# A one-core decoder layer in split float32: the last two products of each column of weight blocks in the same order as all others

## The chip, the core and the metric

The kernel runs on one core of a Trainium2 chip, as one program. The metric is the device time of one execution in microseconds (us), the median of three runs. The engines of the core are TensorE (PE in the profile, its weight loads PEld), VectorE (DVE), ScalarE (ACT), GpSimd (POOL) and SyncE (SP, which starts the transfers).

## What is computed

One layer of a hybrid decoder on 256 tokens of width 2048, in float32: a combined projection, two kinds of attention, gates, an output projection, a wide feed-forward part with a convolution of width 3, and a gated embedding at the end. Cut to what matters here, it is a chain of matrix products:

```python
u = rmsnorm(h, g_mix_pre)
proj = u @ w_in                       # q, k, v of 16 heads, two gates
ya = dilated_mixture_attention(...) @ w_branch_a
yb = stick_breaking_attention(...) @ w_branch_b
mix = (sigmoid(gla) * ya + sigmoid(glb) * yb) @ w_out
h = h + rmsnorm(mix, g_mix_post)
u = rmsnorm(h, g_ffn_pre)
up = causal_depthwise_conv(u @ w_up, conv_w, conv_b)
f = (gelu(gate_ff) * value) @ w_down
h = h + rmsnorm(f, g_ffn_post)
h = h + sigmoid(h @ w_ple_gate) * (p @ w_ple_in)
```

## The kernel before

**Split products.** Every float32 factor is held as two parts of a shorter kind (fp32r): a high part, and a low part that is the rest. ACT rounds (L124 for weights, L284 for activations), DVE subtracts (L127, L290, L292). A product of an activation with a weight is high x high + low x high + high x low. An activation tile (u, mg, ft, yT) has for each of its rows k 256 columns of high parts and, behind them, 256 columns of low parts, 512 in all.

**Blocks, columns, tiles.** A weight block is 128x128. The plan lists them in the order in which PE uses them; eight blocks make a tile of 128x1024, which SP loads (raw), ACT turns into hi and DVE into lo. There are 508 tiles, 4064 blocks. All blocks that add up to the same 128 outputs are a column: 16 blocks for most projections, 11 for each quarter of the down projection.

**A block's products.** For most blocks the function mul makes two products. The high one takes the weights' high part against all 512 columns and fills a whole PSUM bank of 512 columns; the low one takes the weights' low part against the first 256 columns and adds to the first half of the bank. Blocks but the last do the high product (L205) and then the low one (L206). The last block of a column does the low one first (L202) and then the high one (L203). mul1 (the branch products, each part's very last column, the small e products; L223 to L225) makes three products of 256 columns, and the v projection three of 512 with the roles exchanged (L436 to L438).

**Order around it.** PE runs the plan in order, column behind column. `mm` is one column; `several` and the loops over a group `first`, `up` or `pg` run three or four columns side by side, row by row, and so end with their last blocks next to each other. A column has a bank of its own, one of four to seven that go round. When a column is done, `both` copies the bank's second half away on ACT (L247) and lets DVE add it to the first half (L250); what follows goes on from there in stages that a queue (`defer`, `due`) hands out, one stage each time PE's program comes to a new tile (`tick`). Ahead of each column's first product PE waits until its bank has been emptied, and ahead of each tile until ACT and DVE have made it. ACT and DVE wait until the buffer that they fill (seven of each) is no longer read.

Of the kernel before, what the change touches and what calls it, by code (L numbers as in the profile page):

```python
# [14 lines left out]
T = 256  # L15
# [77 lines left out]
def hybrid_block_kernel(ctx: ExitStack, tc: tile.TileContext, gx, pT, convp, bias, masks, w, out):  # L93
    nc = tc.nc
    PE, DVE, ACT = nc.tensor, nc.vector, nc.scalar
# [84 lines left out]
    def block(n=1):  # L180

        b = at["block"]
        at["block"] = b + n
        i, c = divmod(b, 8)
        if c == 0:
            tick(i)
        return hi[i][:, c * 128:(c + n) * 128], lo[i][:, c * 128:(c + n) * 128]
# [10 lines left out]
    def mul(ps, rhs, first, last):  # L198

        wh, wl = block()  # L200
        if last:
            PE.matmul(ps[:, :T], wl, rhs[:, :T], start=False, stop=False, skip_group_check=True)  # L202
            PE.matmul(ps, wh, rhs, start=first, stop=True, skip_group_check=True)  # L203
        else:
            PE.matmul(ps, wh, rhs, start=first, stop=False, skip_group_check=True)  # L205
            PE.matmul(ps[:, :T], wl, rhs[:, :T], start=False, stop=False, skip_group_check=True)  # L206

    head = []

# [19 lines left out]
    def bank():  # L229
        pool, bufs = banks["of"][banks["n"] % len(banks["of"])]  # L230
        banks["n"] += 1
        return pool.tile([128, 2 * T], F32, name="mm", bufs=bufs)

    def mm(key, src, fn=mul, ps=None):

        ps = bank() if ps is None else ps
        for _, k, first, last in group(key):
            fn(ps if fn is mul else ps[:, :T], src[:, k], first, last)
        return ps
# [138 lines left out]
    for c, k, first, last in todo:  # L378
        if k == 6:
            at["grow"] = 0.5  # L380
        if c == 0 and 0 < k < KT - 2:
            usplit(u, k + 2, h[:, k + 2], gain(0, k + 2))
        if first:
            mul_first(pss, c, u[:, k])
            continue
        mul(pss[c], u[:, k], first, last)
# [28 lines left out]
    for c in range(len(pss), 8):  # L415
        ps = mm(keys[c], u, ps=spare.pop(0) if spare else None)
# [111 lines left out]
    for s in range(NS):  # L528
        for c in range(8 if s else 0):
            ps = mm(("qk", s, c), u)  # L530
# [46 lines left out]
    for j in range(KT):  # L577
        ps = bank()
# [11 lines left out]
    def several(key, n, src):  # L590
        pss = [bank() for _ in range(n)]
        for c, k, first, last in group(key):
            mul(pss[c], src[:, k], first, last)
        return pss
# [12 lines left out]
    ps = mm(("out", KT - 1), mg, mul1)  # L607
# [103 lines left out]
    for q in range(NQ):  # L711
        for n in range(max(len(pss), q * 2 * QT), (q + 1) * 2 * QT):
            ps = mm(keys[n], u2)
# [4 lines left out]
        for j in range(KT):  # L718
            if q == NQ - 1 and j == KT - 1:
                break  # L720
            ps = down[j] if j < 3 else mm(("down", q, j), ft)
# [7 lines left out]
    ps = mm(("down", NQ - 1, KT - 1), ft, mul1)  # L729
# [24 lines left out]
    for j in range(KT):  # L754
        ps = pss[j] if j < FIRST else mm(("pg", j), u3, mul1 if j == KT - 1 else mul)
# [67 lines left out]
```

## Time and profile before

| what | value |
|---|---|
| median of three runs | 1485.17 us (1484.68 to 1486.23) |
| the profiled execution, whole | 1486.11 us |
| its span, first to last instruction | 1484.3 us |
| PE busy | 1471.9 us, 99% of the span |
| PE's weight loads busy | 1283.7 us, 86% |
| DVE busy | 1035.6 us, 70% |
| ACT busy | 813.0 us, 55% |
| high products on L205 that read u: count, mean | 2448, 400 ns |
| low products on L206 that read u: count, mean | 2448, 281 ns |

The profile lists one execution. Matmuls overlap: a product is listed from its start to its end, and the next one starts before that end, so that the distance from start to start is shorter than the duration. The time that a product costs is therefore read from the starts. A line in order of time has the start, the duration, the engine, the line of the kernel, the operation and its tiles; in brackets stands how long the engine had been idle before it and what released it.

### The profile page before, as it was taken

To read this page: it belongs to the slowest core of one execution; us is meant where nothing else is said; L and a number is where in the kernel's file an instruction comes from. 1 tells how busy PE (TensorE), PEld (TensorE's weight loads), DVE (VectorE), ACT (ScalarE), POOL (GpSimd) and SP (SyncE) were. 2 spreads that over 40 slices of the span, in tenths; PEclk is the share of its full clock that TensorE was granted. 3 is DMA by queue.
4 is the path that set the end of the run, shared out by engine and by line. 5 is a ranking of instruction groups with operands and counts; after the bars stand their busy time and mean duration, and the time that the engine had idled before them with its cause. 6 is when DMAs were issued, how large, how long until landed. Compare 5 with 4: busy or idle time off the path is not lost.

```text
span 1484.3 us, 21918 instructions
## 1 busy us (share of the span) xinstructions
PE 1471.9 (99%) x8425; PEld 1283.7 (86%) x8425; DVE 1035.6 (70%) x1533; ACT 813.0 (55%) x1215; POOL 22.6 (2%) x30
## 2 busy tenths in 40 slices
PE   8999999999999999999999999999999999999998
PEld 7888888888998988978888888888888888888887
DVE  7665555566666655599965778767787677777884
ACT  7454545464455555566654555545555455656562
POOL 0000000000000000020000000000000000000200
PEclk9999999999999999999999999999999999999999
DMA  9645555566566666545765665665656665656381
GB/s 327 214 158 171 174 183 175 182 196 189 187 188 185 185 187 184 168 157 168 221 194 186 185 189 183 192 186 184 186 185 188 191 186 185 185 185 187 111 272 54
DMA packets 78295, 275.11 MB, mean 185 GB/s; under 512 B 8688, under 2 KB 11632, under 8 KB 78192
## 3 DMA queue, kind: packets, MB, share of 16 engines
q1 hardware_dynamic: 78192, 273.73, 59.4%
q8 instruction: 66, 1.08, 0.3%
q14 instruction: 37, 0.30, 0.1%
HBM read 271.60 MB, written 2.10 MB: 184 GB/s over the span
## 4 chain that ended last, share of the span: by engine, by line
PE 96%; DVE 3%; DMA 0%; issue 0%; ACT 0%; SPq 0%
PE mm L205 51%; PE mm L206 26%; PE mm L203 4%; PE mm L436 2%; PE mm L438 2%; PE mm L437 2%; PE mm L202 2%; PE mm L224 1%; PE mm L225 1%; PE mm L223 1%; DVE lo L127 1%; DVE gh L638 1%; PE S L455 1%; PE S L205 0%; DMA raw<-in_w 0%; DVE u L292 0%
## 5 line engine op out<-in xcount | busy, mean ns | idle before, releaser
L205 PE MATMUL mm<-u,hi 128*128 128x512 f32 x2448 | 875.1, 400 | 4.1 <-DVE u L292 2.6
L127 DVE TENSOR_TENSOR lo<-raw,hi 128x1024 fp32r<-128x1024 f32 (+1 forms) x510 | 622.9, 1227 | 182.0 <-ACT hi L124 174.3
L206 PE MATMUL mm<-u,lo 128*128 128x256 f32 x2448 | 688.2, 281 | 0.5 <-DVE lo L127 0.5
L124 ACT ACTIVATE hi<-raw 128x1024 fp32r<-128x1024 f32 (+1 forms) x510 | 534.6, 1053 | 257.6 <-PE mm L205 195.7
L205 PEld LDWEIGHTS mm<-u,hi 128*128 128x128 f32 x2448 | 461.4, 188 | 112.7 <-DVE u L292 3.6
L206 PEld LDWEIGHTS mm<-u,lo 128*128 128x128 f32 x2448 | 463.7, 189 | 6.5 <-DVE lo L127 1.0
L247 ACT ACTIVATE t<-mm 128x256 f32<-128x256 f32 x242 | 91.4, 378 | 248.3 <-PE mm L203 247.9
L205 PE MATMUL mm<-ft,hi 128*128 128x512 f32 x630 | 224.7, 398 | 0.0
L250 DVE TENSOR_TENSOR s<-mm,t 128x256 f32<-128x256 f32 x211 | 89.1, 422 | 129.8 <-ACT t L247 129.8
L206 PE MATMUL mm<-ft,lo 128*128 128x256 f32 x630 | 176.8, 281 | 0.0
L205 PEld LDWEIGHTS mm<-ft,hi 128*128 128x128 f32 x630 | 118.5, 188 | 26.6
L206 PEld LDWEIGHTS mm<-ft,lo 128*128 128x128 f32 x630 | 119.0, 189 | 2.5
L205 PE MATMUL mm<-mg,hi 128*128 128x512 f32 x225 | 80.0, 399 | 0.0
L203 PE MATMUL mm<-u,hi 128*128 128x512 f32 x164 | 65.0, 399 | 0.0
L206 PE MATMUL mm<-mg,lo 128*128 128x256 f32 x225 | 63.2, 281 | 0.0
L693 ACT ACTIVATE cv<-cpad,cw 128x256 f32<-128x256 f32 x88 | 52.6, 598 | 9.1 <-DVE cpad L688 8.7
L436 PE MATMUL mm<-hi,u 128*128 128x512 f32 x128 | 51.1, 400 | 0.0
L205 PEld LDWEIGHTS mm<-mg,hi 128*128 128x128 f32 x225 | 42.3, 188 | 9.9
L438 PE MATMUL mm<-hi,u 128*128 128x512 f32 x128 | 49.9, 390 | 0.0
L437 PE MATMUL mm<-lo,u 128*128 128x512 f32 x128 | 49.8, 389 | 0.0
L202 PE MATMUL mm<-u,lo 128*128 128x256 f32 x164 | 46.3, 282 | 0.0
L697 DVE SCALAR_TENSOR_TENSOR cv<-cpad,cw,cv 128x256 f32<-128x256 f32 x88 | 42.7, 485 | 3.1
(195 smaller groups left out, 1221.1 us busy)
## 6 DMA issues: line engine op xcount, KB each, us to landing
raw<-in_w SPq DMA_DIRECT2D x507, 512.0 KB, 3.6
bi<-in_bias SPq DMA_DIRECT2D x4, 576.0 KB, 4.8
out<-t SPq DMA_DIRECT2D x16, 128.0 KB, 4.1
gh<-in_gx SPq DMA_DIRECT2D x7, 256.0 KB, 7.0
mk<-in_masks SPq DMA_DIRECT2D x1, 320.0 KB, 6.3
raw<-in_w SPq DMA_DIRECT2D x2, 128.0 KB, 2.5
raw<-in_w SPq DMA_DIRECT2D x1, 256.0 KB, 3.3
t<-in_pT SPq DMA_DIRECT2D x2, 128.0 KB, 5.6
```

The costliest lines, as they stand in the source:

```text
L124: ACT.activation(hi[i][:, a:b], raw[i][:, a:b], AF.Copy)
L127: DVE.tensor_tensor(lo[i][:, a:b], raw[i][:, a:b], f(hi[i][:, a:b]), OP.subtract)
L202: PE.matmul(ps[:, :T], wl, rhs[:, :T], start=False, stop=False, skip_group_check=True)
L203: PE.matmul(ps, wh, rhs, start=first, stop=True, skip_group_check=True)
L205: PE.matmul(ps, wh, rhs, start=first, stop=False, skip_group_check=True)
L206: PE.matmul(ps[:, :T], wl, rhs[:, :T], start=False, stop=False, skip_group_check=True)
L247: ACT.activation(t1[0], ps[:, T:], AF.Copy)
L250: DVE.tensor_tensor(out, ps[:, :T], t1[0], OP.add)
L436: PE.matmul(pv[t], xh, wh, start=kt == 0, stop=False)
L437: PE.matmul(pv[t], xh, wl, start=False, stop=False)
L438: PE.matmul(pv[t], xl, wh, start=False, stop=kt == KT - 1)
L693: ACT.activation(y, c[:, 2:], AF.Identity, scale=cw[:, n, 2:3], bias=cw[:, n, 3:4])
```

## The change

The branch for a column's last block goes. The last block does the high product first and the low one last, as all other blocks do. Both products of the last block now carry the mark that ends an accumulation. The number and the sizes of the products stay the same; four lines fewer shift all later line numbers (L205 and L203 become L201, L206 and L202 become L202, L247 becomes L243).

```diff
     def mul(ps, rhs, first, last):
 
         wh, wl = block()
-        if last:
-            PE.matmul(ps[:, :T], wl, rhs[:, :T], start=False, stop=False, skip_group_check=True)
-            PE.matmul(ps, wh, rhs, start=first, stop=True, skip_group_check=True)
-        else:
-            PE.matmul(ps, wh, rhs, start=first, stop=False, skip_group_check=True)
-            PE.matmul(ps[:, :T], wl, rhs[:, :T], start=False, stop=False, skip_group_check=True)
+        PE.matmul(ps, wh, rhs, start=first, stop=last, skip_group_check=True)
+        PE.matmul(ps[:, :T], wl, rhs[:, :T], start=False, stop=last, skip_group_check=True)
```

PE's order where one column of the up projection ends (bank mm_6902) and the next begins (mm_6958), before; in brackets are the engines that a product waits for.

```order
L205 MATMUL mm_6902<-u2_5863,hi_6764 128x512
L206 MATMUL mm_6902<-u2_5863,lo_6765 128x256
L202 MATMUL mm_6902<-u2_5863,lo_6765 128x256
L203 MATMUL mm_6902<-u2_5863,hi_6764 128x512
L205 MATMUL mm_6958<-u2_5863,hi_6794 128x512 [waits PE_49,Activation_49]
L206 MATMUL mm_6958<-u2_5863,lo_6795 128x256 [waits DVE_49]
```

The same place after.

```order
L201 MATMUL mm_6902<-u2_5863,hi_6764 128x512
L202 MATMUL mm_6902<-u2_5863,lo_6765 128x256
L201 MATMUL mm_6902<-u2_5863,hi_6764 128x512
L202 MATMUL mm_6902<-u2_5863,lo_6765 128x256
L201 MATMUL mm_6958<-u2_5863,hi_6794 128x512 [waits PE_49,Activation_49]
L202 MATMUL mm_6958<-u2_5863,lo_6795 128x256 [waits DVE_49]
```

Low, low, high, high has become high, low, high, low. PE's order in the first quarter of the down projection, where the last rows of three columns (mm_7294 to mm_7296) stand side by side, before.

```order
L205 MATMUL mm_7296<-ft_6186,hi_7212 128x512
L206 MATMUL mm_7296<-ft_6186,lo_7213 128x256
L202 MATMUL mm_7294<-ft_6186,lo_7213 128x256 [waits Activation_49]
L203 MATMUL mm_7294<-ft_6186,hi_7212 128x512 [waits DVE_49]
L202 MATMUL mm_7295<-ft_6186,lo_7213 128x256
L203 MATMUL mm_7295<-ft_6186,hi_7212 128x512
L202 MATMUL mm_7296<-ft_6186,lo_7243 128x256
L203 MATMUL mm_7296<-ft_6186,hi_7242 128x512
```

The same place after.

```order
L201 MATMUL mm_7296<-ft_6186,hi_7212 128x512
L202 MATMUL mm_7296<-ft_6186,lo_7213 128x256
L201 MATMUL mm_7294<-ft_6186,hi_7212 128x512 [waits DVE_49]
L202 MATMUL mm_7294<-ft_6186,lo_7213 128x256
L201 MATMUL mm_7295<-ft_6186,hi_7212 128x512
L202 MATMUL mm_7295<-ft_6186,lo_7213 128x256
L201 MATMUL mm_7296<-ft_6186,hi_7242 128x512
L202 MATMUL mm_7296<-ft_6186,lo_7243 128x256
```

Here three exchanges in a row are gone, and the first product of the last row is the one that waits for DVE's half of ft.

## Rows read from the trace of the kernel before

**Rows 1.** The page: its first line of busy times, the granted clock by slices, and the chain that ended last by engine.

```profile
PE 1471.9 (99%) x8425; PEld 1283.7 (86%) x8425; DVE 1035.6 (70%) x1533; ACT 813.0 (55%) x1215; POOL 22.6 (2%) x30
...
PEclk9999999999999999999999999999999999999999
...
PE 96%; DVE 3%; DMA 0%; issue 0%; ACT 0%; SPq 0%
```

**Rows 2.** The waits, longest first in total: who waited for whom, us in all, how often, the longest.

```profile
ACT t L247 <- PE mm L203: 247.9, 151, 4.4
...
PE mm L205 <- DVE u L292: 2.6, 5, 0.6
```

**Rows 3.** PE in order of time in the up projection, the last high products (L203) of four columns: start us, us, engine, line, operation. From 837.67 to 945.09 there are 19 columns. Then, by line, the high products of L205 in a stretch of the column that ends at 832.03 and in one of the column behind 837.67: count, durations in ns (least, median, greatest), first and last start.

```profile
826.46 0.40 PE L203 MATMUL mm<-u,hi 128*128 128x512 f32 x1
...
832.03 0.40 PE L203 MATMUL mm<-u,hi 128*128 128x512 f32 x1
...
837.67 0.40 PE L203 MATMUL mm<-u,hi 128*128 128x512 f32 x1
...
945.09 0.40 PE L203 MATMUL mm<-u,hi 128*128 128x512 f32 x1
...
L205 PE MATMUL mm<-u,hi x12: 391/391/391, 827.7 to 831.6; 128*128 128x512 f32 x12
...
L205 PE MATMUL mm<-u,hi x15: 395/398/403, 837.9 to 842.8; 128*128 128x512 f32 x15
```

**Rows 4.** The products of L203 in the banks mm, by the tile that they read: count, durations in ns (least, median, greatest), first and last start. Three more stand in the banks S and po.

```profile
L203 PE MATMUL mm<-u,hi x164: 387/400/400, 31.7 to 1474.3; 128*128 128x512 f32 x164
...
L203 PE MATMUL mm<-ft,hi x63: 392/396/400, 769.7 to 1376.0; 128*128 128x512 f32 x63
...
L203 PE MATMUL mm<-mg,hi x15: 396/400/403, 548.9 to 617.4; 128*128 128x512 f32 x15
```

**Rows 5.** All engines in order of time around the end of one gate column.

```profile
337.41 0.28 PE L206 MATMUL mm<-u,lo 128*128 128x256 f32 x1
...
337.52 0.28 PE L202 MATMUL mm<-u,lo 128*128 128x256 f32 x1
337.53 0.19 PEld L203 LDWEIGHTS mm<-u,hi 128*128 128x128 f32 x1
337.64 0.40 PE L203 MATMUL mm<-u,hi 128*128 128x512 f32 x1
...
337.88 0.40 PE L205 MATMUL mm<-u,hi 128*128 128x512 f32 x1
...
338.11 0.28 PE L206 MATMUL mm<-u,lo 128*128 128x256 f32 x1
...
338.14 0.38 ACT L247 ACTIVATE t<-mm 128x256 f32<-128x256 f32 x1 [1.94 <-PE mm L203]
```

**Rows 6.** The same view at the first down projection: DVE's half of the last row of ft, then PE from the next-to-last row (a high and a low product for each of three banks in turn) to the start of the last row, and the last high products of two down columns, eight columns apart.

```profile
764.25 0.42 DVE L290 TENSOR_TENSOR ft<-cv,ft 128x256 fp32r<-128x256 f32 x1
...
768.74 0.28 PE L206 MATMUL mm<-ft,lo 128*128 128x256 f32 x1
...
768.86 0.40 PE L205 MATMUL mm<-ft,hi 128*128 128x512 f32 x1
...
769.57 0.28 PE L202 MATMUL mm<-ft,lo 128*128 128x256 f32 x1
...
956.74 0.40 PE L203 MATMUL mm<-ft,hi 128*128 128x512 f32 x1
...
987.77 0.40 PE L203 MATMUL mm<-ft,hi 128*128 128x512 f32 x1
```

**Rows 7.** PE in order of time: two high products (L205), ten pairs apart, behind each of three kinds of other matmuls: behind the sums of squares (L337) of the first part, behind a branch product (L225), and behind the sums of squares ahead of the long part.

```profile
45.36 0.39 PE L205 MATMUL po<-u,hi 128*128 128x512 f32 x1
...
48.82 0.39 PE L205 MATMUL po<-u,hi 128*128 128x512 f32 x1
...
360.83 0.40 PE L205 MATMUL mm<-u,hi 128*128 128x512 f32 x1
...
364.37 0.40 PE L205 MATMUL mm<-u,hi 128*128 128x512 f32 x1
...
669.21 0.40 PE L205 MATMUL mm<-u,hi 128*128 128x512 f32 x1
...
672.75 0.40 PE L205 MATMUL mm<-u,hi 128*128 128x512 f32 x1
```

**Rows 8.** The last high products (L203) before and at the end of two columns: one among the q and k columns, one in the final projection.

```profile
124.38 0.40 PE L203 MATMUL mm<-u,hi 128*128 128x512 f32 x1
...
129.94 0.40 PE L203 MATMUL mm<-u,hi 128*128 128x512 f32 x1
...
1417.83 0.40 PE L203 MATMUL mm<-u,hi 128*128 128x512 f32 x1
...
1423.39 0.40 PE L203 MATMUL mm<-u,hi 128*128 128x512 f32 x1
```

**Rows 9.** All engines at the eighth block of a tile, whose high product lets a buffer go.

```profile
334.69 0.40 PE L205 MATMUL mm<-u,hi 128*128 128x512 f32 x1
...
334.94 0.28 PE L206 MATMUL mm<-u,lo 128*128 128x256 f32 x1
...
335.13 1.06 ACT L124 ACTIVATE hi<-raw 128x1024 fp32r<-128x1024 f32 x1 [1.04 <-PE mm L205]
```

## The prediction

> **What bounds the kernel now.** I read the page's busy shares first, then the chain of work that ended last, then the waits, then the matmuls in order of time. The page shows PE busy 99% of the span at a granted clock of 9 tenths or more in every slice (the level of 2.4 GHz), and PE is 96% of the chain [rows 1]. Waits of PE are small: the products of L205 wait 2.6 us in all for a half of u, while the 247.9 us that ACT waits for L203 are an engine off the bound waiting for PE [rows 2]. So the time is the sum of the distances between the starts of successive matmuls, and an edit counts only if it moves those distances or makes PE wait.
>
> One thing more must be seen there. From pair to pair (high product, then low product) there is not one distance but two. Ten pairs from 45.36 to 48.82 take 0.346 us each, ten from 669.21 to 672.75 take 0.354 [rows 7]. The view by line shows it too: the high products of L205 in the column that ends at 832.03 are all listed at 391 ns, those in the column behind 837.67 at 395 to 403 [rows 3]. I call these the fast and the slow tempo. Within a column I found no change of tempo; it changes at ends of columns and where other matmuls stand between. A fast column of 16 blocks takes 832.03 - 826.46 = 5.57 us, a slow one (945.09 - 837.67) / 19 = 5.654 us, 0.353 a pair [rows 3]. Of the 4064 blocks most run slow: in the long part with the up and down projections four columns are fast (the one that ends at 832.03 is one), all others slow.
>
> **The change, part by part.** Counts: the last product of a column by mul is made 164 + 63 + 15 times and three times more in other banks [rows 4], 245 in all; that many exchanges go. Nothing is added.
>
> *The exchange itself.* Before, the starts run low 337.41, low (last) 337.52, high (last) 337.64, next column's high 337.88: 0.11 + 0.12 + 0.24 = 0.47 us. After, the same place reads low, high, low, high: a regular high product is followed after 0.23 us (337.88, 338.11) [rows 5], a regular low one after 0.12 (768.74, 768.86) [rows 6], 0.12 + 0.23 + 0.12 = 0.47 us. A start follows a product of 512 columns by 0.23 to 0.24 us and one of 256 by 0.11 to 0.12, whatever comes next; I take 0 and keep -0.005 to +0.005 us a column, -1.2 to +1.2 us in all.
>
> *Who waits at a column's end.* ACT's L247 copies the upper half of the bank and starts at 338.14, 0.50 us after the last high product [rows 5]. After, the low product ends the column: it starts 0.23 us behind the high one and is listed at 0.28 us, so its end stands 0.51 us behind the high start; now the high product's end stands 0.12 + 0.40 = 0.52 us behind the low start. ACT, and DVE's sum behind it, move by 0.01 us. Nobody on PE waits for them: the bank comes round again only some columns (5.6 us each) later. 0.
>
> *The activations.* The exchanged order begins a last row with the low product, which needs only ACT's half of u or ft; now the high product comes first and needs DVE's half too. That half of ft is there at 764.25 + 0.42 = 764.67 us and the last row begins at 769.57 [rows 6]: 4.9 us of cover. If it were gone, at most the 0.12 us of a low product would be lost, at the few places where a row is fresh. 0.
>
> *Buffers of weights.* A high tile is let go 0.12 us sooner and a low tile 0.24 us later at a column's end. ACT and DVE fill them some tiles ahead, and a tile lasts 8 x 0.35 = 2.8 us. 0; if that cover were gone, 0.24 us a tile would be the price.
>
> *Tempo.* This is the term with a size. Each exchange breaks the alternation (low, low, high, high), and the tempo changes at such breaks: the column that ends at 832.03 is fast between slow ones [rows 3]. Without breaks I expect a stretch to keep the tempo with which it starts, until other matmuls interrupt. The starts seen: behind a branch product pairs from 360.83 to 364.37 take 0.354 us each, slow; behind the sums of squares ahead of the long part, from 669.21 to 672.75, slow; behind the sums of squares of the first part, from 45.36 to 48.82, 0.346, fast [rows 7].
>
> So most likely the long part stays slow, and the fast columns that breaks made are lost, each 5.654 - 5.57 = 0.084 us: seven in the gates, three among the q and k columns without attention work ahead, four in the up part, one at the end, 15 in all by their starts (first 124.38 to 129.94, last 1417.83 to 1423.39 [rows 8]), 15 x 0.084 = 1.3 us. The down columns of 11 blocks take (987.77 - 956.74) / 8 = 3.879 us [rows 6]; 11 slow pairs would be 5.654 x 11/16 = 3.887, so 0.008 x 51 = 0.4 us more. One early column should turn fast, -0.1. Sum: +1.6 us.
>
> The profiled execution took 1486.11 us (span 1484.3 and 1.8 around it), 0.94 us above the median of the runs. With +1.6 us it would take 1487.7; on the median, 1485.17 + 1.6 = **1486.8 us**. A measurement of this kernel can tell about 0.2%, 3.0 us, so this is no change that can be told.
>
> **Rivals.**
> *The long part locks into the fast tempo.* If the start behind the sums ahead of the long part comes out fast, nothing interrupts from 669 to 1376 us: 707 us, some 2000 pairs, each 0.007 us shorter (0.353 against 0.346): -14 us, with the other terms about 1473 us. For it: the start at 45.36 came out fast. Against it: the one at 669.21 came out slow [rows 7]; but both places are entered a little differently after the change, so neither binds. Chance 0.17. If it broke off midway, the time would lie between.
>
> *The next weights lie open (slower).* Now the first high product of a column stands behind a product of 512 columns, 0.24 us; after, behind one of 256, 0.12 us. Its weight load is listed at 0.19 us [rows 5]. If the load, together with the column's first wait for a bank, can't start early, 0.19 - 0.12 = 0.07 us open at each of 245 columns: +17 us, 1502 us; it decides from 0.012 us a column. Against it: every regular low product is followed by a high one after 0.12 us with the same load, also where the bank changes (low 768.74, high 768.86 of the next column) [rows 6]. Chance 0.06, most of it far below 17 us.
>
> *Signals.* At a column's end both products now have to signal, the high one that its weights are free and the low one that the bank is ready. The high product at 334.69 releases ACT at 335.13, and the next start follows after 0.25 us [rows 9] against 0.23 to 0.24 elsewhere: 0.01 us x 245 = 2.5 us, 1489.3 with the terms above. The Trainium skill, page "TensorE: Matmul & The Clock Gate", section "The cost: per-tile semaphore tail", says that increments serialize and gives about 26.3 ns for each; by that, as an estimate, 245 x 26.3 ns = 6.4 us. The row shows less than half of that. Chance 0.05.
>
> That the change doesn't do what it says is excluded by the program's order, where the ends of columns read high, low.
>
> **How the numbers follow.** Forecast (slow tempo, -1 to +3 us): 0.72. Fast lock 0.17, open loads 0.06, signals 0.05. Faster by over 0.2% is the fast lock, 0.17; slower by over 0.2% is the last two, 0.11; within, 0.72. The forecast's own range is 1484.0 (its small terms at their lower ends) to 1488.1; signals reach 1489.3. From 1484.0 to 1489.0 lie the forecast's 0.72 and the nearer parts of the last two cases, 0.8; the fast lock is left out, since it lies far off.
>
> **What would show it.** Right: high products of the long part listed at 395 to 403 ns, columns 5.65 us apart, no new wait of PE, ACT's copy 0.5 us behind the last high product. The fast lock: 391 ns over hundreds of us and columns of 5.55 us. Open loads: the first high product of a column starting more than 0.12 us behind the low one. Wrong altogether: a third tempo, or a wait of PE on DVE or ACT at a column's end.

## The result, and the profile after

The kernel after takes **1472.03 us** (median of 20 runs, 1469.94 to 1486.28), the kernel before 1485.01 us (20 runs, 1484.19 to 1487.19): ratio 0.994, 95% interval 0.9924 to 0.9957. It is faster, by 13 us or 0.9% at the medians. The forecast was 1486.8 us, no change that can be told; the time lies 12 us under the low end of its range and 1 us from the first rival, to which a chance of 0.17 was given.

The spread of the 20 runs tells more than their median. Thirteen lie at 1469.94 to 1472.75 us, seven at 1483.32 to 1486.28, none between. One program has two times, 13 to 14 us apart, and the kernel before had only the upper one. The granted clock does not tell them apart: it was 0.999 to 1.000 in every one of the 20 runs.

The profiled execution of after took 1471.94 us, so it shows the lower time. Its page, the lines that answer to [rows 1]:

```profile
PE 1456.4 (99%) x8425; PEld 1279.8 (87%) x8425; DVE 1035.2 (70%) x1533; ACT 812.9 (55%) x1215; POOL 22.6 (2%) x30
...
PEclk9999999999999999999999999999999999999999
...
PE 96%; DVE 3%; DMA 0%; issue 0%; ACT 0%; SPq 0%
PE mm L201 54%; PE mm L202 28%; PE mm L432 2%; PE mm L434 2%; PE mm L433 2%; PE mm L221 1%; PE mm L220 1%; PE mm L219 1%; DVE lo L127 1%; DVE gh L634 1%; PE S L451 1%; PE S L201 0%; DMA raw<-in_w 0%; DVE u L288 0%; PE po L505 0%; DVE u L286 0%
```

Nothing has moved there: PE is busy 99% at the same granted clock and is 96% of the chain. All high products of mul are L201 now, all low ones L202 (other lines stand 4 lower than before). The waits that answer to [rows 2] are as before too:

```profile
ACT t L243 <- PE mm L202: 239.4, 148, 4.4
...
PE mm L201 <- DVE u L288: 2.1, 4, 0.6
```

What moved is the distance between starts. By line, the high products of the long part (count, least, median and greatest duration in ns, first and last start), against the 395 to 403 of its slow columns in [rows 3]:

```profile
L201 PE MATMUL mm<-u,hi x1311: 391/391/391, 667.2 to 1304.4; 128*128 128x512 f32 x188
...
L201 PE MATMUL mm<-ft,hi x693: 391/391/391, 755.6 to 1361.6; 128*128 128x512 f32 x174
```

All 2004 behind its first one are at 391 ns, least and greatest alike: the long part runs in the fast tempo from its first pair to its last. From the high product behind the sums of squares (666.67) to the last high product of ft (1361.6) are 694.9 us, 0.3467 a pair; before, from 668.33 to 1376.0, it was 707.7. That is 12.8 of the 14.1 us between the two spans. The part ahead is 1.7 us shorter and the part behind 0.3 longer; the part ahead varies by that much between executions of the same code (in the profiles of x_once, two6, two7 and split1 below, which share it with after, that product starts at 667.4 to 669.6).

PE at the entry of the long part in time, for [rows 7]:

```profile
665.65 0.40 PE L201 MATMUL mm<-u,hi 128*128 128x512 f32 x1
...
666.67 0.59 PE L201 MATMUL mm<-u,hi 128*128 128x512 f32 x1
667.10 0.28 PE L202 MATMUL mm<-u,lo 128*128 128x256 f32 x1
667.22 0.39 PE L201 MATMUL mm<-u,hi 128*128 128x512 f32 x1
...
670.68 0.39 PE L201 MATMUL mm<-u,hi 128*128 128x512 f32 x1
```

Ten pairs behind the sums take 670.68 - 667.22 = 3.46 us, 0.346 each, where they took 0.354 before. The other long streams stayed slow: high products of the first gate pair (the two gate columns) behind a branch, of out (the product with w_out), and of the last product (pg, with w_ple_gate), by line:

```profile
L201 PE MATMUL mm<-u,hi x31: 395/398/403, 329.9 to 340.5; 128*128 128x512 f32 x31
...
L201 PE MATMUL mm<-mg,hi x238: 395/398/403, 531.1 to 614.8; 128*128 128x512 f32 x119
...
L201 PE MATMUL mm<-u,hi x145: 395/398/403, 1407.0 to 1457.8; 128*128 128x512 f32 x145
```

### The profile page after: what moved, and what is told of

Same layout as the page of the kernel before. It is cut to its first block, busy times and chain, and to the rows that moved or that the text cites. A ratio compares the mean times of both kernels' runs of the same rounds, so it can differ in the third digit from the quotient of the medians.

```text
span 1470.2 us, 21918 instructions
## 1 busy us (share of the span) xinstructions
PE 1456.4 (99%) x8425; PEld 1279.8 (87%) x8425; DVE 1035.2 (70%) x1533; ACT 812.9 (55%) x1215; POOL 22.6 (2%) x30
## 4 chain that ended last, share of the span: by engine, by line
PE 96%; DVE 3%; DMA 0%; issue 0%; ACT 0%; SPq 0%
PE mm L201 54%; PE mm L202 28%; PE mm L432 2%; PE mm L434 2%; PE mm L433 2%; PE mm L221 1%; PE mm L220 1%; PE mm L219 1%; DVE lo L127 1%; DVE gh L634 1%; PE S L451 1%; PE S L201 0%; DMA raw<-in_w 0%; DVE u L288 0%; PE po L505 0%; DVE u L286 0%
## 5 line engine op out<-in xcount | busy, mean ns | idle before, releaser
L201 PE MATMUL mm<-u,hi 128*128 128x512 f32 x2612 | 917.4, 395 | 5.1 <-DVE u L288 2.1
L202 PE MATMUL mm<-u,lo 128*128 128x256 f32 x2612 | 731.6, 280 | 0.8 <-DVE lo L127 0.8
L201 PEld LDWEIGHTS mm<-u,hi 128*128 128x128 f32 x2612 | 489.5, 187 | 119.6 <-DVE u L288 3.6
L202 PEld LDWEIGHTS mm<-u,lo 128*128 128x128 f32 x2612 | 493.4, 189 | 1.1 <-DVE lo L127 1.1
L201 PE MATMUL mm<-ft,hi 128*128 128x512 f32 x693 | 240.4, 391 | 0.0
L243 ACT ACTIVATE t<-mm 128x256 f32<-128x256 f32 x242 | 91.4, 378 | 239.9 <-PE mm L202 239.4
L202 PE MATMUL mm<-ft,lo 128*128 128x256 f32 x693 | 194.0, 280 | 0.0
L201 PEld LDWEIGHTS mm<-ft,hi 128*128 128x128 f32 x693 | 129.6, 187 | 28.4
L202 PEld LDWEIGHTS mm<-ft,lo 128*128 128x128 f32 x693 | 131.0, 189 | 0.0
L201 PE MATMUL mm<-mg,hi 128*128 128x512 f32 x240 | 84.8, 399 | 0.0
L202 PE MATMUL mm<-mg,lo 128*128 128x256 f32 x240 | 67.4, 281 | 0.0
L201 PEld LDWEIGHTS mm<-mg,hi 128*128 128x128 f32 x240 | 45.1, 188 | 11.2
L202 PEld LDWEIGHTS mm<-mg,lo 128*128 128x128 f32 x240 | 45.3, 189 | 0.0
L693 DVE SCALAR_TENSOR_TENSOR cv<-cpad,cw,cv 128x256 f32<-128x256 f32 x88 | 42.7, 485 | 3.1
L692 DVE SCALAR_TENSOR_TENSOR cv<-cpad,cw,cv 128x256 f32<-128x256 f32 x88 | 42.1, 478 | 0.0
```

The source lines that it names most:

```text
L201: PE.matmul(ps, wh, rhs, start=first, stop=last, skip_group_check=True)
L202: PE.matmul(ps[:, :T], wl, rhs[:, :T], start=False, stop=last, skip_group_check=True)
L243: ACT.activation(t1[0], ps[:, T:], AF.Copy)
L692: DVE.scalar_tensor_tensor(y, c[:, 1:T + 1], cw[:, n, 1:2], y, op0=OP.mult, op1=OP.add)
L693: DVE.scalar_tensor_tensor(y, c[:, 0:T], cw[:, n, 0:1], y, op0=OP.mult, op1=OP.add)
```

## The experiments

**Theories.** *Tempo*: the time is set by the tempo in which the one uninterrupted stream of the long part (2005 pairs; the expectations below say 2001) runs; a stream keeps its tempo until something breaks the alternation of high and low, and such a break can turn it either way. *Price*: each of the 245 exchanges costs something by itself, 13 us / 245 = 0.053 us. *Run*: the two times come from something in a run that has nothing to do with the order.

All kernels are the kernel after with a few blocks changed; a block is one pair of products, numbered from the start of a stream (`at[key]` lists the blocks of a group, `ends` takes the last of each column). "The long part" starts at the first block of column 6 of up. The common edit, in which `swaps` is the set of exchanged blocks:

```diff
 def mul(ps, rhs, first, last):
+    swap = at["block"] in swaps
     wh, wl = block()
+    if swap:
+        PE.matmul(ps[:, :T], wl, rhs[:, :T], start=False, stop=False, skip_group_check=True)
+        PE.matmul(ps, wh, rhs, start=first, stop=last, skip_group_check=True)
+        return
     PE.matmul(ps, wh, rhs, start=first, stop=last, skip_group_check=True)
```

The kernels x_, those from two6 to split1, those from lock_slow to all_fast, and all_word ran on one chip each with the kernel before, whose medians were 1485.31, 1485.23, 1485.22 and 1484.99 us. "Low" counts runs at 1469.9 to 1475.5 us, "high" those at 1483 to 1489.1; no run lay between. The last two kernels lie at 1466.4 to 1470.7, at the lower edge of low and under it.

| kernel | exchanges | runs | low | high | median us | ratio to before, 95% |
|---|---|---|---|---|---|---|
| after | 0 | 20 | 13 | 7 | 1472.03 | 0.9924 to 0.9957 |
| x_long | 145 in the long part | 11 | 0 | 11 | 1484.81 | 0.9986 to 1.0004 |
| x_rest | 100 elsewhere | 12 | 7 | 5 | 1472.92 | 0.9923 to 0.9974 |
| x_once | 1 | 12 | 3 | 9 | 1485.15 | 0.9959 to 1.0003 |
| x_word | 6 | 4 | 4 | 0 | 1472.91 | 0.9901 to 0.9927 |
| two6 | 2, six blocks apart | 12 | 7 | 5 | 1475.15 | 0.9933 to 0.9982 |
| two7 | 2, seven apart | 12 | 4 | 8 | 1483.99 | 0.9946 to 0.9998 |
| gate_pos | 14 in the gates | 1 | | 1 | 1483.81 | |
| split1 | 0, one block split | 12 | 3 | 9 | 1485.99 | 0.9951 to 1.0001 |
| lock_slow | 0, eight split | 11 | 0 | 11 | 1486.19 | 0.9997 to 1.0014 |
| lock_fast | 1, eight split | 6 | 5 | 1 | 1474.34 | 0.9910 to 0.9937 |
| all_fast | 17, sixteen split | 4 | | | 1468.90 | 0.9877 to 0.9904 |
| all_word | 38 | 4 | | | 1467.52 | 0.9864 to 0.9897 |

**x_long and x_rest: the two halves of the change.**

```diff
+    long = [k for k in at if k[0] == "down" or k[0] == "up" and k[1] >= FIRST + 2]
+    return ends(long)                                # x_long: last blocks of these columns
+    return ends([k for k in at if k not in long])    # x_rest: of all the others
```

> The kernel after, with the 145 exchanges of the long part alone put back (columns 6 to 87 of up and the 63 of down). Tempo theory: an exchange met in the fast tempo ends it and the other 144, fifteen pairs apart, keep the slow one, so the 2001 pairs of the long part take 353 ns instead of 347: about 1485 us in every run, the long part slow in the profile, and none of the runs at 1470 to 1473. Price theory (every exchange costs the same 13 us / 245 = 0.053 us wherever it stands): 1472.0 + 145 x 0.053 = 1479.7 us.

> The kernel after, with the 100 exchanges outside the long part put back and none in it. Tempo theory: the long part runs without an exchange as in the kernel after, in the tempo in which it is entered: most runs at 1470 to 1473 us, perhaps some at 1483 to 1486, none between. Price theory: 1472.0 + 100 x 0.053 = 1477.3 us.

Measured: x_long 1484.81 us with no run under 1483.19, x_rest 1472.92 with both levels (1471.02 to 1473.13 and 1484.97 to 1486.82). The whole effect comes from the 145 exchanges of the long part, and the other 100 do nothing that can be told. Price asked for 1479.7 and 1477.3; neither median is near, and no run is.

**x_once: one exchange.**

```diff
+    return {at["up", FIRST + 2][-1][0]}
```

> The kernel after, with a single exchange in it, at the end of column 6 of up, the first column of the long part. Tempo theory: where the long part was entered fast, this one exchange turns it slow, where it was entered slow it stays slow, and nothing turns it back in the 1985 pairs behind it: about 1484 to 1486 us in every run. Price theory: 1472.0 + 0.05 = 1472.1 us, with the two levels of the kernel after.

Nine of 12 runs at 1484.57 to 1488.63, where after had seven of 20. Shares of so few runs don't settle it; the profiled run does, and ends the price theory: in it **one exchanged pair among some 4000 costs 13 us**. The high products of column 6 ahead of the exchange, and all behind it, by line:

```profile
L218 PE MATMUL mm<-u,hi x15: 391/391/587, 667.4 to 672.4; 128*128 128x512 f32 x15
...
L218 PE MATMUL mm<-u,hi x1294: 394/398/404, 673.8 to 1317.2; 128*128 128x512 f32 x185
L218 PE MATMUL mm<-ft,hi x693: 394/398/404, 757.9 to 1375.5; 128*128 128x512 f32 x174
```

Fourteen at 391 or 392 ns and the one behind the sums (587), the exchange at 672.9, and then 1987 at 394 to 404 ns without a way back. The expectation missed one thing: three runs came out low. The share of low runs of after (13 of 20) and x_rest (7 of 12) has turned over, as if the exchange made a stream that was entered slow fast. None of the three was profiled.

**x_word: six exchanges.**

```diff
+    start = at["up", FIRST + 2][0][0]
+    return {start + n for n in (1, 7, 14, 20, 27, 33)}
```

> The kernel after, with six exchanges at the start of the long part (its blocks 1, 7, 14, 20, 27 and 33). By the places in the stream at which exchanges of the kernel before turned the slow tempo into the fast one, this row of distances (6, 7, 6, 7, 6) leads into the fast tempo from the fast one and from each of the slow one's three positions. Tempo theory: 1470 to 1473 us in every run, with no run at 1483 to 1486. Price theory: 1472.0 + 6 x 0.053 = 1472.3 us as a median, with the two levels of the kernel after. If the two levels come from something in a run other than the order of the products, about a third of the runs lies at 1483 to 1486.

Four of four low. With 20 of the 32 runs of after and x_rest low anyway, that alone is not enough (0.62^4 = 0.15); all_word below adds four. The profiled run was entered fast, went slow at blocks 1, 14 and 27, and fast again at 7, 20 and 33.

**two6 and two7: the same two exchanges, one block moved.**

```diff
+    return {start + n for n in (15, 21)}    # two6
+    return {start + n for n in (15, 22)}    # two7
```

> The kernel after, with two exchanges in the long part, at its blocks 15 and 21, six blocks apart. Tempo theory, as x_once left it: each single exchange at a fitting place turns the tempo over. Entered fast (about two runs in three), the first one makes it slow and the second, six blocks (two of the slow tempo's three-block rounds) later, fast again: 1471 to 1474 us. Entered slow, the first makes it fast and the second slow: 1484 to 1487. So the two levels of the kernel after, with about its shares, and 1472 us as the median. Price theory: the same as the kernel after, 1472.1 us.

> The same two exchanges, but the second at block 22 of the long part, seven blocks behind the first. Tempo theory: entered fast, the first exchange makes the tempo slow and the second meets it at a place of the three-block round from which it does not turn: slow to the end. Entered slow, the first makes it fast and the second slow. About 1484 to 1488 us in every run, 13 us above two6 for a second exchange that stands one block later. Price theory: no difference to two6.

The shares differ in the expected direction (7 of 12 low against 4 of 12), but so few runs can't tell them apart, and two7 was expected without low runs. Its profiled run is one of them (1472.14 us, span 1470.4), and shows why: high products ahead of the first exchange and the last of them, between the two and the last of these, and behind the second, by line:

```profile
L219 PE MATMUL mm<-u,hi x13: 395/398/582, 668.0 to 672.5; 128*128 128x512 f32 x13
...
L219 PE MATMUL mm<-u,hi x1: 398/398/398, 673.2 to 673.2; 128*128 128x512 f32 x1
...
L219 PE MATMUL mm<-u,hi x5: 387/396/403, 674.2 to 675.6; 128*128 128x512 f32 x5
...
L219 PE MATMUL mm<-u,hi x1: 395/395/395, 675.6 to 675.6; 128*128 128x512 f32 x1
...
L219 PE MATMUL mm<-u,hi x1282: 391/391/392, 678.8 to 1305.9; 128*128 128x512 f32 x184
```

It was entered slow. The first exchange, behind a product of 398 ns, left it slow; the second, behind one of 395, turned it fast. In two6 the profiled run was entered fast, ran slow between the exchanges and fast behind them:

```profile
L219 PE MATMUL mm<-u,hi x14: 391/391/586, 669.6 to 674.3; 128*128 128x512 f32 x14
...
L219 PE MATMUL mm<-u,hi x5: 393/395/403, 675.3 to 676.7; 128*128 128x512 f32 x5
...
L219 PE MATMUL mm<-u,hi x1286: 390/391/392, 678.8 to 1307.3; 128*128 128x512 f32 x184
```

So the entry is open in each run, and from either entry the places of the exchanges lead on. What failed is the expectation that a stream entered slow is turned fast by the exchange at block 15: from this entry it came at a place that doesn't turn.

**gate_pos: the place scanned in 14 streams at once.**

```diff
+    return {at["ga", j][1 + (j - LATE) % 7][0] for j in range(LATE, KT)}
```

> The kernel after, with one exchange in each of the 14 gate pairs that follow a branch: in the first gate column, at block 1, 2, 3, 4, 5, 6, 7, 1, 2, ... from pair to pair. In the kernel after all 14 pairs run slow to their end. Tempo theory with the three-block round: the pairs whose exchange is at block 1, 4 or 7 (pairs 1, 4, 7, 8, 11 and 14) turn fast behind it, the other eight stay slow. Rival: where the exchange stands makes no difference, and all 14 pairs, or none, turn.

High products behind the exchange in pairs 1 to 7, that is with the exchange at block 1, 2, ... 7, by line:

```profile
L218 PE MATMUL mm<-u,hi x24: 391/391/391, 333.3 to 341.3; 128*128 128x512 f32 x24
...
L218 PE MATMUL mm<-u,hi x24: 395/398/403, 347.3 to 355.4; 128*128 128x512 f32 x24
...
L218 PE MATMUL mm<-u,hi x24: 391/391/391, 362.2 to 370.2; 128*128 128x512 f32 x24
...
L218 PE MATMUL mm<-u,hi x19: 391/391/391, 376.9 to 383.1; 128*128 128x512 f32 x19
...
L218 PE MATMUL mm<-u,hi x26: 395/398/403, 388.4 to 397.6; 128*128 128x512 f32 x26
...
L218 PE MATMUL mm<-u,hi x19: 391/391/391, 405.8 to 412.0; 128*128 128x512 f32 x19
...
L218 PE MATMUL mm<-u,hi x17: 391/391/391, 419.8 to 425.3; 128*128 128x512 f32 x17
```

(The fifth stretch begins two products ahead of its exchange.) At blocks 2 and 5 the stream stays slow, at 1, 3, 4, 6 and 7 it turns, and pairs 8 to 14 repeat the seven. That blocks 3 and 6 turn was not expected. But the number of the block is not the place in the round: pairs 3, 6, 10 and 13, each behind a pair that stayed slow, begin the round at another place than the rest. The last high product ahead of the exchange, in pairs 2, 3, 5 and 6:

```profile
L218 PE MATMUL mm<-u,hi x1: 403/403/403, 345.6 to 345.6; 128*128 128x512 f32 x1
...
L218 PE MATMUL mm<-u,hi x1: 396/396/396, 360.1 to 360.1; 128*128 128x512 f32 x1
...
L218 PE MATMUL mm<-u,hi x1: 403/403/403, 388.8 to 388.8; 128*128 128x512 f32 x1
...
L218 PE MATMUL mm<-u,hi x1: 395/395/395, 403.3 to 403.3; 128*128 128x512 f32 x1
```

All ten exchanges that turned the stream stand behind a product of 395 or 396 ns, all four that didn't behind one of 403. So the place decides, and one place of the three turns, as the theory had it. The three durations of the slow tempo (395, 398, 403) are its three places. This run's long part was entered slow (1483.81 us).

**All exchanges in all profiles.** Taken over the 14 profiles, the exchanges with four regular pairs ahead of them and five behind follow one rule without an exception ("behind a 395" means behind a high product listed nearest to 395 ns): met in the fast tempo, 26 of 26 made it slow; met slow behind a 395, 50 of 50 made it fast; behind a 398, 69 of 69, and behind a 403, 246 of 246, left it slow. (Three more met a stream that ran 392 and 395 in turn, behind a 392, and left it fast.) The rule also says why before runs slow. Behind an exchange that leaves the stream slow the round begins anew, and the distance to the next exchange, 16 or 11 blocks, fixes the place at which it comes: of the 137 exchanges of the long part of before that don't follow directly on another, 104 stand behind a 403 and 27 behind a 398. Three stand behind a 395, and the fast column behind each of them ends at the next exchange.

**split1: a break without an exchange.** The last block of column 6 in the form of the branch products:

```diff
+    if split:
+        PE.matmul(ps[:, :T], wh, rhs[:, :T], start=first, stop=False, skip_group_check=True)
+        PE.matmul(ps[:, T:], wh, rhs[:, T:], start=False, stop=last, skip_group_check=True)
+        PE.matmul(ps[:, :T], wl, rhs[:, :T], start=False, stop=last, skip_group_check=True)
+        return
```

> The kernel after, with one block of the long part changed, the last of column 6 of up: its high product of 512 columns is issued as two of 256 columns on the same weights, ahead of the low one. No order is exchanged; the starts behind it are shifted. Theory A, that any shift of the starts against the rhythm picks the tempo anew: behind the branches, where the same form stands, the tempo came out slow in all 14 pairs, so entered fast it turns slow, 1484 to 1487 us in two runs of three or more. Theory B, that only the exchanged order turns the tempo: the two levels of the kernel after with its shares, median 1472 us.

Three of 12 low, nine high: the shares of x_once, not those of after. This speaks for A, that a shifted start is what matters and the order only one way to shift it. But 12 runs of two levels don't settle it, and the profiled run was entered slow, so that it can't show a split that turns a fast stream. gate_pos shows that eight blocks in this form do: its pair 1 ends at 391 ns, and behind the branch products, without an exchange, pair 2 begins slow:

```profile
L218 PE MATMUL mm<-u,hi x26: 391/391/391, 333.3 to 342.0; 128*128 128x512 f32 x26
...
L218 PE MATMUL mm<-u,hi x2: 396/400/403, 345.2 to 345.6; 128*128 128x512 f32 x2
```

**lock_slow and lock_fast: the tempo set on purpose.** Blocks 1 to 8 of the long part split as in split1, and in lock_fast an exchange at block 10:

```diff
+    return set(), set(range(start + 1, start + 9))            # lock_slow: swaps, splits
+    return {start + 10}, set(range(start + 1, start + 9))     # lock_fast
```

> The kernel after, with eight blocks of the long part (1 to 8 of its first column, column 6 of up) issued in the branch products' form: the high product as two of 256 columns, then the low one. No exchange anywhere. Tempo theory: behind eight such blocks the stream begins slow, as behind each of the 14 branches, whatever it was before, and nothing turns it in the 1990 pairs behind: 1484 to 1488 us in every run. Rival, that the two levels come from something in a run other than the stream of starts: two runs in three at 1470 to 1473.

> The same eight blocks, and one exchange, at block 10, the second one behind them, as gate_pos had it in its pairs 1 and 8. Tempo theory: slow behind the eight, turned fast by the one exchange, and fast to the end: 1470 to 1474 us in every run, 13 us under lock_slow for one exchanged pair. Rival as before: the same two levels as in lock_slow, with the same shares. Price theory: 0.05 us above lock_slow.

lock_slow: 11 of 11 high. lock_fast: five of six low, with the median 12 us under it for one exchanged pair. This ends the run theory as it stood: eight split blocks bring all of 11 runs to the upper level, and one exchanged pair behind them leaves one of six there. The one high run of lock_fast (1485.93 us) was the profiled one. Behind the exchange it is slow to the end:

```profile
L224 PE MATMUL mm<-u,hi x1301: 393/398/404, 671.4 to 1317.3; 128*128 128x512 f32 x186
```

So eight split blocks leave the stream slow but not always at the same place, and one exchange misses it then: the pair ahead of it is listed at 397 and 278 ns here, the same pair of lock_slow at 397 and 282.

**all_fast and all_word: every long stream.**

```diff
+    swaps = {at["ga", j][1][0] for j in range(LATE, KT)} | {out + 1, long + 10, pg + 10}
+    return swaps, {s + n for s in (long, pg) for n in range(1, 9)}                        # all_fast
+    starts = [at["first"][16][0], at["up", FIRST + 2][0][0], at["out"][0][0], at["pg", FIRST][0][0]]
+    swaps = {at["ga", j][1][0] for j in range(LATE, KT)}
+    return swaps | {s + n for s in starts for n in (1, 7, 14, 20, 27, 33)}                # all_word
```

> lock_fast, and the same done in the other streams that run slow in the kernel after: an exchange at block 1 of the first column of each of the 14 gate pairs and at block 1 of out, which stand right behind branch products, and eight blocks and one exchange at the start of the fifth column of the last product. Tempo theory, 6.7 ns a pair: 14 x 30 pairs 2.8 us, some 230 pairs of out 1.5 us, some 165 pairs of the last product 1.1 us where it had been slow, against lock_fast: 1466 to 1469 us in every run, which beats both kernels. Rival: no less than lock_fast.

> x_word's six exchanges (blocks 1, 7, 14, 20, 27 and 33 of a stream) in place of the eight split blocks and one exchange, at the start of four streams: the second half of the first product, the long part, out, and the fifth column of the last product; and one exchange at block 1 of the first column of each of the 14 gate pairs, as in all_fast. Tempo theory, if six exchanges lead into the fast tempo from every place as they did in the four runs of x_word: gates 2.8 us, out 1.3, the first product 0.3, the last product 1.0 against x_word: 1466 to 1469 us in every run, as all_fast or up to 1 us under it, since no block is split. If the row of distances found at column ends does not hold inside columns, x_word's four runs were luck (two runs in three are entered fast anyway), and some runs here lie near 1480. Price theory: 38 x 0.053 = 2 us over the kernel after.

all_fast 1468.90 us (1466.47 to 1470.67), 5.4 us under lock_fast, where 2.8 + 1.5 + 1.1 were expected. all_word **1467.52 us** (1466.45 to 1469.09): 17.5 us under before, and the fastest here. In its profile a gate column, out, the long part and the last product, by line, all stand at 390 to 392 ns:

```profile
L220 PE MATMUL mm<-u,hi x25: 391/391/392, 389.6 to 398.0; 128*128 128x512 f32 x25
...
L220 PE MATMUL mm<-mg,hi x200: 390/391/392, 544.7 to 613.6; 128*128 128x512 f32 x100
...
L220 PE MATMUL mm<-u,hi x1275: 390/391/392, 677.9 to 1302.6; 128*128 128x512 f32 x183
L220 PE MATMUL mm<-ft,hi x693: 390/391/392, 753.9 to 1359.8; 128*128 128x512 f32 x174
...
L220 PE MATMUL mm<-u,hi x138: 390/391/392, 1409.6 to 1457.1; 128*128 128x512 f32 x138
```

In x_word and all_word together no run of eight was high; 20 low runs in 32 would give that in 2 cases of 100. Both profiles were entered fast. Worked through with the rule above and the rounds seen behind exchanges, the row of six ends fast from each of the three slow places too; no profile shows that.

**What decides the entry.** The profiles answer a question that no kernel was built for. In the kernels without an exchange in the blocks ahead of the sums, the last high product ahead of the sums has a listed duration; after, x_once, two7 and gate_pos, by line:

```profile
L201 PE MATMUL mm<-u,hi x1: 398/398/398, 665.6 to 665.6; 128*128 128x512 f32 x1
```

```profile
L218 PE MATMUL mm<-u,hi x1: 398/398/398, 666.3 to 666.3; 128*128 128x512 f32 x1
```

```profile
L219 PE MATMUL mm<-u,hi x1: 395/395/395, 667.0 to 667.0; 128*128 128x512 f32 x1
```

```profile
L218 PE MATMUL mm<-u,hi x1: 395/395/395, 665.4 to 665.4; 128*128 128x512 f32 x1
```

Where the slow round stands at 398 when the four sums come, the long part is entered fast (after, x_once, and also x_long and two6); where it stands at 395, slow (two7, gate_pos, and also split1). Seven of seven profiles agree. So the sums too are a break whose outcome hangs on the place, and the two levels of after are, by these profiles, that place. The third place was met once, in lock_slow (404 ns ahead of the sums), whose split blocks hide what it gives. What sets the place from run to run was not tried.

## Why the prediction was wrong

- **What bounds the kernel**: right. PE is 96% of the chain, and only distances between starts moved.
- **The exchange itself, 0 (-1.2 to +1.2)**: right. x_long, with 145 exchanges and a slow long part, takes 1484.81 us; the seven high runs of after, with none, have the median 1485.17. Four columns that are fast in x_long's profile account for 0.3 us of the difference.
- **Who waits at a column's end, 0**: right. A gate column's end after, in time, all engines, for [rows 5]:

```profile
334.90 0.40 PE L201 MATMUL mm<-u,hi 128*128 128x512 f32 x1
335.13 0.28 PE L202 MATMUL mm<-u,lo 128*128 128x256 f32 x1
335.25 0.40 PE L201 MATMUL mm<-u,hi 128*128 128x512 f32 x1
...
335.51 0.39 ACT L243 ACTIVATE t<-mm 128x256 f32<-128x256 f32 x1 [1.94 <-PE mm L202]
```

  The low product ends 0.23 + 0.28 = 0.51 us behind the high start, as forecast, and ACT's copy follows 0.1 us later, 0.61 behind the high start. The list of what would show it said 0.5 there; that was loose, since the copy stood 0.1 us behind the end before too.
- **The activations, 0**: right. DVE's half of ft is there at 760.90 + 0.42 = 761.32 us, and the last row, 30 pairs of 0.3467 us behind the first start of ft at 755.6, begins at 755.6 + 30 x 0.3467 = 766.0: 4.7 us of cover, forecast 4.9.
- **Open weight loads (rival)**: did not come. 335.25 stands 0.12 us behind the low product, and the 2004 high products of the long part behind its first, with all its column ends among them, keep 391 ns and 0.3467 us a pair.
- **Signals (rival)**: did not come, by the same 391 ns and the same distances: a product that signals is not longer than its neighbours. The section "The cost: per-tile semaphore tail" of the Trainium skill's page "TensorE: Matmul & The Clock Gate" gives about 26.3 ns for each increment in the tail behind a series of tiles; no run here shows that inside PE's stream.
- **Tempo**: here it failed, and in one step: "So most likely the long part stays slow". That a stretch keeps its tempo until other matmuls interrupt was right (x_once, 1987 pairs), and so was the size of the rival: -14 us was given for 707 us of stream, 12.8 were measured between the profiles. Wrong was to read the entry off the one profile of before, where an exchange stood right ahead of the sums, and to hold the start behind the sums for a property of that place. It depends on where the round of three stands (398 ahead of the sums in after, fast), and by the times it comes out fast in 13 of 20 runs. The rows spoke of it: breaks turned a stream both ways, and a start behind the sums of the first part was fast. The two entries seen, one of each kind, bore out a chance near one half; 0.17 was the mis-sized number. The other thing not seen was that before could not be fast for long, since it met an exchange every 16 or 11 blocks, and one ends the fast tempo (26 of 26): its slow tempo was a product of the exchanges, not the tempo of the stream. So the forecast of a slow long part rested on a start that the change itself removed.
- **Lost fast columns, +1.6**: the 14 gate pairs behind a branch run slow in the profile of after, as forecast. In the runs whose long part stays slow the time is 1485.17 us, 0.2 over before, not 1.6. What makes up for it was not isolated; the last product, slow in the profile of after, is mostly fast in those of x_once, two7 and lock_slow, where the part behind its sums of squares is 1.3 us shorter.

## What to carry to other kernels

Where one engine is busy 99%, read the distances of its starts, not only its waits: a stream of one and the same pair of matmuls ran here at 391 or at 395 to 403 ns a high product for 700 us, and one pair in another order, or one place earlier or later, decided which. Ask of each edit what it does to the rhythm that it leaves behind, and run a kernel with such a stream often enough to see both levels: three runs of after could all have come from one of them. To get the better level, put breaks where they lead into it, as x_word and all_word did in eight runs of eight, instead of hoping for the entry.

## What the runs showed of the hardware

- Two tempos of the same stream of f32r products (512 and 256 columns in turn) at the same granted clock (9 tenths or more in every slice, the level of 2.4 GHz): 0.3467 us a pair with all high products at 391 ns (after, 2004 pairs), and 0.3533 with 395, 398 and 403 in turn (x_once, 1987 pairs). Neither changes by itself in 700 us. In short stretches a third listing occurs, 392 and 395 in turn, at the fast distance (after, 321.53 to 326.04: 13 pairs of 0.347 us).
- The slow tempo has a round of three pairs, and the outcome of a break hangs on the place in it. An exchange turns the slow tempo fast behind a 395 (50 of 50) and leaves it slow behind a 398 or a 403 (315 of 315); met in the fast tempo it makes it slow (26 of 26). By the entries above, four sums of squares turn it fast behind 398 and leave it slow behind 395.
- In before the exchanges at the ends of columns kept the long part slow but for a few columns, and x_long, with the same ones, ran at the upper level 11 times of 11; in all_word exchanges 6 and 7 blocks apart led into the fast tempo in all four runs. Why there are two tempos, and what sets the place at which a run comes to the sums, stays open.
